# A fused two-block transformer kernel: modulation products on TensorE, weight loads one unit later, and an mLSTM loop fetched ahead through the sync queue

## The chip, the core and the metric

The kernel runs on one core of a Trainium2 chip. The metric is the device time of one launch in microseconds (us), and the time given for a kernel is the median of its runs. PE is TensorE, PEld its weight loads, DVE is VectorE, ACT is ScalarE, POOL is GpSimd, and SP is SyncE, which here does nothing but issue transfers.

## What is computed

The sequence has 512 tokens of width 1024. The first block is a hybrid mixer (a gated delta rule and an mLSTM, each run in both directions over chunks of 64 tokens) with a mixture of experts behind it; the second, run twice, is an attention layer with a feed-forward part. Each block is steered by six modulation vectors, which come from a short vector `c` and a wide matrix:

```
c_act = jax.nn.silu(c.astype(jnp.float32))
...
mod = c_act @ ada_w[l].astype(jnp.float32) + ada_b[l].astype(jnp.float32)
sh1, sc1, gt1, sh2, sc2, gt2 = [m[:, None, :] for m in jnp.split(mod, N_MOD, axis=-1)]
hn = rmsnorm(h_res, norm_mix_g[l]) * (1.0 + sc1) + sh1
h_res = h_res + gt1 * hybrid_mixer(
...
```

In the mixer one wide projection feeds everything; the two branches are computed from it and merged under a gate:

```
proj = jnp.einsum("bsd,de->bse", h, w_in.astype(jnp.float32))
a_qkv, a_z, a_gates, b_qk, b_v, b_o, b_gates, merge = jnp.split(proj, SPLIT_POINTS, axis=-1)
...
o_a = rmsnorm(o_a, gdn_norm_g) * jax.nn.silu(a_z.reshape(bsz, s, N_HEADS_A, HEAD_DIM_A))
...
h_b = head_layernorm(h_b, mlstm_norm_g.astype(jnp.float32).reshape(N_HEADS_B, HEAD_DIM_B))
h_b = (h_b * jax.nn.sigmoid(b_o.reshape(bsz, s, N_HEADS_B, HEAD_DIM_B))).reshape(bsz, s, WIDTH_B)
gate_a, gate_b = jnp.split(jax.nn.sigmoid(merge), 2, axis=-1)
y = (gate_a * jnp.einsum("bse,ed->bsd", o_a, w_branch_a.astype(jnp.float32))
     + gate_b * jnp.einsum("bse,ed->bsd", h_b, w_branch_b.astype(jnp.float32)))
```

## The kernel before

**Products.** Activations lie with features on the partitions and 512 tokens along the free axis. Every weight and every activation of a large product is split into a high and a low part, and a product is three matmuls: high by high, high by low, low by high. A weight tile of 1 MB arrives by a transfer of SP into one of four buffers named `raw`; `_split` takes a unit of 1024 columns out of it, ACT copies it to `whi`, and POOL subtracts to get `wlo` (`lo_pool` says whether POOL, 1, or DVE, 0, does that; it is `(1,)` in the mixer). `unit` hands out the next unit, `_ahead` splits up to two units ahead of it, and `_loads` issues loads while fewer than four tiles are held. The matmuls of such units write PSUM tiles named `pd` (128x512) or `tm` (128x256).

**Main and fill.** The mixer's order is that of the program. `drive` runs a main generator, which earns credit, and spends the credit on steps of a fill generator. The main one is first the gated delta rule, twice (directions: half the heads each time): preparation (`pl`, `ptr`, `pG`), a triangular elimination that is a long row of small DVE operations (`stmp<-L,Tm` and `Tm<-Tm,stmp`, the sweep), a block solve (`pQ`, `pY`, `pw`, `pu`), and a scan over chunks in which PE and DVE take turns (`pS`, `pv`). Then it is the mLSTM loop. The fill is the rest of the wide projection: its results go to DRAM by way of tiles `stg` (`z_d`, `qk_d`, `v_d`, `o_d`, and the merge gates `mg_d`) and are fetched again later. Into the fill `weave` puts a step of the modulation work whenever 4.2 units of fill have gone by.

**Modulation.** `ada` (three groups of eight units here: two of the first block, one of the second) takes a `raw` tile of 1024 by 256 and multiplies row block k by column k of `c`. ACT scales four of the eight blocks in place, DVE multiplies and adds the other four into `adacc`, POOL adds ACT's four together and onto `adacc`, and PE sums over the partitions with a vector of ones (`pa`). At the very start of the kernel `ada_first` already does the same product for one group on PE alone (`pada`, column blocks of 32). The buffer `raw` is free for the next load when POOL is done.

**mLSTM loop.** `mlstm` has 16 steps: four pairs of heads, four blocks of 128 keys. A step multiplies queries and keys (`pqk`), DVE multiplies the result by decay weights (`rowt`), and PE multiplies that with the values (`pm`). The weights of a step are a row fetched from DRAM (`mdram`) and spread over the partitions, masked by POOL (`affine_select`) and put through Exp by ACT. After four steps a pair of heads is normalised, gated with the output gate `og` in `mlstm_out`, transposed (`pht`) and split. The fetches of `rowt` are issued by the scalar queue (ACT's), three steps ahead; `og` is fetched when `mlstm_out` begins. Ahead of them on the scalar queue stands the fetch of `oa`, the result of the first branch, which was stored to DRAM just before. Behind the fill, `branch_in` splits `oa` and `branch_a` multiplies it by `wa`, gate by gate (`mg`); both are steps of the fill too.

Of the kernel before, what the change touches and what calls it, by code (L numbers as in the profile page):

```python
# [175 lines left out]
class Build:  # L176
# [151 lines left out]
    def unit(self, key, sel):  # L328

        i = len(self.order)  # L330
        self.order.append((key, sel))
        if self.order_in is None:
            self.raws = getattr(self, "raws", {})
            if key not in self.raws:
                self.raws = {key: self._load(key)}
            self.ready = getattr(self, "ready", {})
            return (i,) + self._split(i)
        assert self.order_in[i] == (key, sel), (i, self.order_in[i], key, sel)
        self._ahead(i)
        return (i,) + self.ready.pop(i)  # L340
# [116 lines left out]
    def ada(self, w, c, bias, out, groups, eng=None):  # L457
# [3 lines left out]
        for g in groups:  # L461
# [915 lines left out]

    def mlstm(self, mp, qk, v_d, o_d, oh, ol):

# [3 lines left out]
        steps = [(f, a) for f in range(4) for a in range(4)]  # L1383
        rowt = {}

        def fetch(i):
            if i < len(steps):
                f, a = steps[i]
                t = rowt[i] = mp.tile([P, 2, 640], F32, tag="rowt", bufs=5, name="rowt")
                self.dma("scalar", t, self.mdram[2 * f:2 * f + 2, a, :].partition_broadcast(P))  # L1390

        def weights(i):
            if i < len(steps):
                f, a = steps[i]
                t, n = rowt[i], T - P * a
                for d in range(2):
                    dg = t[:, :, T:] if d else t[:, :, 0:P]
                    sg = -1 if d else 1
                    nc.gpsimd.affine_select(dg, dg, pattern=[[0, 2], [sg, P]], compare_op=OP.is_ge, fill=NEG, base=0, channel_multiplier=-sg)
                for hh in range(2):  # L1400
                    for d, r in ((0, t[:, hh, 0:n]), (1, t[:, hh, n:])):
                        self.act(r, r, AF.Exp, bias=self.rcol[:, d, a, 2 * f + hh:2 * f + hh + 1])

        va = mp.tile([P, 4, 8, 65], F32, name="va")
        for i in range(4):
            if i < 3:
                fetch(i)
            self.dma("sync", va[:, i], v_d[:, i])
        self.mlg = self.big_row(mp, "ml_g")
        for i in range(2):  # L1410
            weights(i)
        out = None
        for i in range(len(steps) + 1):
            if i < len(steps):
# [5 lines left out]
                for hh in range(2):  # L1420
                    for d in range(2):
                        _, n, t0 = self.span(d, a)
                        r = rowt[i][:, hh, 0:n] if d == 0 else rowt[i][:, hh, 640 - n:]
                        self.stt(r, pss[hh][:, t0:t0 + n], 0.125, r, OP.mult, OP.mult)
            fetch(i + 3)
            weights(i + 2)
            yield 0.6
            if i > 0:
                f, a = steps[i - 1]
                r = rowt.pop(i - 1)  # L1430
                if a == 0:
                    po = [[self.pc("pm") if hh == 0 else self.pd("pm") for _ in range(2)] for hh in range(2)]
# [7 lines left out]
                if a == 3:  # L1440
# [16 lines left out]
                    self.drain(out)  # L1457
                    out = self.mlstm_out(mp, f, hs, o_d, oh, ol)
            for _ in range(3):
# [4 lines left out]

    def mlstm_out(self, mp, f, hs, o_d, oh, ol):

        nc = self.nc
        sh = [P, 4, 2, 64]
        og = mp.tile([P, 4, P], F32, tag="og", bufs=1, name="og")
        self.dma("sync", og, o_d[:, :, P * f:P * f + P])  # L1470
        sm, ss = [mp.tile([P, 4, 2], F32, tag=f"ls{i}", bufs=2, name="ls") for i in range(2)]
# [45 lines left out]

    def branch_in(self, oa, hi, lo):

        for k in range(4):  # L1520
            self.split(oa[:, k], hi[:, k], lo[:, k])
        yield 0.0
# [1046 lines left out]
    def mixer(self, mod0, mod1, px):  # L2569
# [3 lines left out]
        md = lambda i: mod0[:, 8 * i:8 * i + 8]  # L2573
        ada0 = lambda gs: self.ada("ada0", c1, self.vc("ada_b0"), mod0, gs, nc.gpsimd)
        with tc.tile_pool(name="x0", bufs=1, reuse_waits="tile") as x0:
# [45 lines left out]
        self.marks = set()  # L2621
        ada = self.chain(ada0((1, 2)), self.ada("ada1", c2, self.vc("ada_b1"), mod1, (0,), nc.gpsimd))
        with tc.tile_pool(name="mb", bufs=1, reuse_waits="tile") as mb:
            with tc.tile_pool(name="ms", bufs=1, reuse_waits="tile") as ms:
# [4 lines left out]
                with tc.tile_pool(name="mq", bufs=1, reuse_waits="tile") as mq:  # L2629
# [36 lines left out]
            def place():  # L2666
                ya.extend(self.h_tile(m % 2, 4 + m // 2, F32) for m in range(KD))
                yield 0.0

            with tc.tile_pool(name="mp", bufs=1, reuse_waits="tile") as mp:  # L2670
                oa = mp.tile([P, 4, T], F32, name="oa")
                self.dma("scalar", oa, oa_d)
                fill = self.chain(fill, self.branch_in(oa, hi, lo), place(), self.branch_a("wa", (hi[:, 0:4], lo[:, 0:4]), ya, mg_d, mp, 2))
                fill = self.drive(self.mlstm(mp, qk, v_d, o_d, oh, ol), fill)
                self.drain(fill)
        with tc.tile_pool(name="mr", bufs=1, reuse_waits="tile") as mr:
            with ph:
# [127 lines left out]
```

## Time and profile before

| | |
|---|---|
| median of 3 runs | 2731.18 us (2724.32 to 2737.99) |
| profiled execution | 2728.39 us, its span 2726.6 us |
| PE busy | 2490.4 us, 91% of the span |
| DVE, ACT, POOL busy | 1524.1, 929.5, 957.9 us |
| mixer with the mLSTM loop | from about 60 to 745 us of the span |

The page divides the span in 40 slices; the mixer is slices 2 to 11, where PE is mostly 7 or 8 tenths busy and its granted clock below 1 in most slices, while nearly all slices after the 16th show 9 and 9. Times of a stretch are counted from the start of the span. A wait in brackets is the idle time of an engine just before an instruction, with what ended it. Two records of PE stand for one float32 matmul (`pada`, `pa`, `pm`, `pqk`), one for a matmul of split parts (`pd`, `tm`).

### The profile page before, as it was taken

The numbers are of one execution on the slowest core, as the hardware profiler recorded it, in microseconds if no ns is written. First come the engines' busy times: TensorE is split into PE (matmuls) and PEld (weight loads), VectorE is DVE, ScalarE is ACT, GpSimd is POOL, SyncE is SP. The second block draws the span as 40 slices with busy tenths as digits, with TensorE's granted clock in tenths as the row PEclk, the third lists the DMA queues.
The fourth block names the chain that finished last, engine by engine and source line by source line (L and its number), as shares of the span: only waits on it lengthen the run. The fifth ranks groups of instructions, "written<-read, shape, count | busy, mean of one in ns | idle before, by whom it ended". The sixth has DMA issues, their size and how long they took to land.

```text
span 2726.6 us, 35040 instructions
## 1 busy us (share of the span) xinstructions
PE 2490.4 (91%) x13618; PEld 1843.4 (68%) x13618; DVE 1524.1 (56%) x2483; ACT 929.5 (34%) x1534; POOL 957.9 (35%) x652
## 2 busy tenths in 40 slices
PE   7888888787969999889999999999999999999999
PEld 4676776566634444557777877878757777888887
DVE  4896595354446645564455488884454345452523
ACT  3434233444222211333444432323332344442432
POOL 1454454332320000443553333444332343344443
PEclk8989898788979999999999999999999999999999
DMA  9356465534389974432446146552331225232321
GB/s 264 93 187 180 150 183 179 203 108 136 102 325 357 391 301 146 135 124 93 146 148 201 63 154 201 170 192 89 102 93 47 85 82 189 78 108 80 106 93 62
DMA packets 332299, 419.07 MB, mean 154 GB/s; under 512 B 33608, under 2 KB 275760, under 8 KB 323680
## 3 DMA queue, kind: packets, MB, share of 16 engines
q1 hardware_dynamic: 312848, 377.12, 41.8%
q10 hardware_dynamic: 14624, 25.28, 2.7%
q0 software_dynamic: 4656, 14.35, 1.6%
q8 instruction: 113, 1.85, 0.3%
q14 instruction: 58, 0.48, 0.1%
HBM read 387.66 MB, written 33.23 MB: 154 GB/s over the span
## 4 chain that ended last, share of the span: by engine, by line
PE 45%; DVE 6%; issue 3%; POOL 2%; ACT 2%; DMA 1%; ACTq 0%; POOLq 0%; DVEq 0%
PE pd L199 36%; PE psc L199 2%; DVE adacc L214 2%; PE tm L199 2%; POOL wlo L205 2%; PE ptot L199 1%; DMA raw<-in_w_up 1%; DVE cv L214 1%; PE po L199 1%; DVE h L214 1%; PE prr L199 1%; PE pc L199 1%; PE pz L199 1%; PE pso L199 1%; PE pst L199 1%
## 5 line engine op out<-in xcount | busy, mean ns | idle before, releaser
L205 POOL TENSOR_TENSOR wlo<-raw,whi 128x1024 fp32r<-128x1024 f32 (+3 forms) x317 | 720.6, 2279 | 1219.3 <-ACT whi L196 1069.6
L199 PE MATMUL pd<-h,whi 128*128 128x512 f32 (+1 forms) x3440 | 1098.6, 401 | 32.9 <-DVE stg L214 6.3
L199 PEld LDWEIGHTS pd<-h,whi 128*128 128x128 f32 x3440 | 646.4, 193 | 191.0 <-issue 27.1
L199 PE MATMUL pd<-h,wlo 128*128 128x512 f32 (+1 forms) x1720 | 675.9, 393 | 21.9 <-POOL wlo L205 21.9
L196 ACT ACTIVATE whi<-raw 128x1024 fp32r<-128x1024 f32 (+3 forms) x319 | 313.9, 993 | 260.4 <-PE pd L199 117.2
L199 PEld LDWEIGHTS pd<-h,wlo 128*128 128x128 f32 x1720 | 331.4, 193 | 94.4 <-POOL wlo L205 26.2
L199 PE MATMUL pd<-fyh,whi 128*128 128x512 f32 (+1 forms) x546 | 204.7, 375 | 9.3 <-ACT whi L196 5.3
L214 DVE SCALAR_TENSOR_TENSOR cv<-pd,vec,cv 128x511 f32<-128x511 f32 (+1 forms) x176 | 131.8, 749 | 143.8 <-ACT cv L196 138.3
L199 PE MATMUL pd<-fyh,wlo 128*128 128x512 f32 (+1 forms) x546 | 201.8, 370 | 5.5 <-POOL wlo L205 5.5
L214 DVE SCALAR_TENSOR_TENSOR adacc<-raw,cs,adacc 128x256 f32<-128x256 f32 x288 | 201.5, 700 | 9.4
L199 PE MATMUL pd<-fyl,whi 128*128 128x512 f32 (+1 forms) x546 | 200.8, 368 | 0.2 <-DVE fyl L205 0.2
L214 DVE SCALAR_TENSOR_TENSOR xTl<-pd,mod,xTl 128x512 f32<-128x512 f32 (+1 forms) x73 | 49.4, 683 | 188.5 <-PE pd L199 188.5
L199 PE MATMUL pgB<-gu,xt 128*64 128x512 f32 (+1 forms) x304 | 143.1, 608 | 0.3 <-PEq L1981 0.3
L199 PE MATMUL pgA<-gu,xt 128*64 128x512 f32 (+1 forms) x304 | 143.2, 608 | 0.0
L199 PE MATMUL tm<-whi,h 128*128 128x256 f32 x640 | 130.7, 297 | 8.3 <-ACT whi L196 7.9
L199 PEld LDWEIGHTS pd<-fyh,whi 128*128 128x128 f32 x546 | 104.6, 192 | 40.1 <-ACT whi L196 10.4
L199 PEld LDWEIGHTS pd<-fyh,wlo 128*128 128x128 f32 x546 | 104.4, 191 | 24.3 <-POOL wlo L205 7.5
L199 PEld LDWEIGHTS pd<-fyl,whi 128*128 128x128 f32 x546 | 104.7, 192 | 16.8 <-DVE fyl L205 0.7
L199 PEld LDWEIGHTS tm<-whi,h 128*128 128x128 f32 x640 | 107.2, 200 | 9.6 <-ACT whi L196 8.2
L199 PE MATMUL tm<-wlo,h 128*128 128x256 f32 x320 | 93.9, 293 | 7.7 <-POOL wlo L205 7.6
L196 ACT ACTIVATE cv<-pd,vec 128x512 f32<-128x512 f32 x88 | 68.2, 775 | 94.5 <-PE pd L199 93.9
L214 DVE SCALAR_TENSOR_TENSOR xT<-pb,mod,xT 128x512 f32<-128x512 f32 x128 | 87.0, 742 | 2.1 <-PE pb L199 1.9
(564 smaller groups left out, 3366.9 us busy)
## 6 DMA issues: line engine op xcount, KB each, us to landing
raw<-in_ada SPq DMA_DIRECT2D x64, 1024.0 KB, 5.4
raw<-in_w_in SPq DMA_DIRECT2D x54, 1024.0 KB, 6.7
raw<-in_w_up SPq DMA_DIRECT2D x44, 1024.0 KB, 4.9
gu<-in_wg SPq DMA_DIRECT2D x30, 1024.0 KB, 8.7
gu<-in_wu SPq DMA_DIRECT2D x30, 1024.0 KB, 7.0
dn<-in_wd SPq DMA_DIRECT2D x59, 512.0 KB, 9.7
raw<-in_w_dn SPq DMA_DIRECT2D x16, 1024.0 KB, 5.1
raw<-in_wo SPq DMA_DIRECT2D x12, 1024.0 KB
```

Source lines behind the costliest of these rows:

```text
L196: return self.nc.scalar.activation(out, in_, func, **kw)
L199: return self.nc.tensor.matmul(out, lhsT, rhs, start=start, stop=stop)
L205: return (eng or self.nc.vector).tensor_tensor(out, a, b, op=op)
L214: return (eng or self.nc.vector).scalar_tensor_tensor(out, a, s, b, op0=op0, op1=op1)
```

## The change

First, `ada_mm` takes the place of `ada` for the three groups in the mixer: PE multiplies the `raw` tile by the broadcast column of `c`, eight products in four column blocks of 32, ACT copies the sum out, and PE folds the four blocks (`pa`). The bias is added once for each group. A step of it counts 1.2 in the credit, and comes after 6.0 units of fill instead of two steps after 4.2 each. The `ada` of the later layers is as it was.

Second, `_loads` is called only at the start of `unit`, no longer after each split and after each `done`, in the whole kernel.

Third, in the mLSTM loop the rows are fetched by SP, four steps ahead; the first step's row is fetched, masked and put through Exp before the loop, in a buffer of its own; `og` is fetched a step before it is used, in two buffers; `oa` comes in four quarters in two buffers, by SP, and is split only when the rest of the fill has run; and `wlo` is made by DVE until the fill has ended.

```
@@ _ahead, _loads, done
             self.nsplit += 1
-            self._loads()
...
                 del self.raws[key]
-                self._loads()
@@ new
+    def ada_mm(self, w, c, bias, out, groups):
+        for g in groups:
+            pcol = self.ps.tile([P, T], F32, tag="a", bufs=self.ps_a, name="pa")
+            pend = None
+            for j in range(9):
+                if j < 8:
+                    u = self.unit((w, 0, KD, 2048 * g + 256 * j, 256), ("raw",))
+                    ps = self.pc("pada")
+                    for k in range(KD):
+                        q = 32 * (k % 4)
+                        self.mm(ps[q:q + 32, 0:256], c[:, k:k + 1].to_broadcast([P, 32]), u[1][:, k, :], k < 4, k >= 4)
+                    self.done(u)
+                if pend is not None:
+                    for i in range(2):
+                        self.mm(pcol[:, 2 * j - 2 + i:2 * j - 1 + i], pend[:, i * P:(i + 1) * P], self.wmean)
+                if j < 8:
+                    pend = self.gp.tile([P, 256], F32, tag="adacc", bufs=2, name="adacc")
+                    self.act(pend, ps[:, 0:256], AF.Copy)
+                    yield 1.2
+            s = slice(16 * g, 16 * g + 16)
+            self.stt(out[:, s], pcol[:, 0:16], float(D), bias[:, s], OP.mult, OP.add)
@@ mlstm
+    def mlstm_fetch(self, t, f, a):
+        self.dma("sync", t, self.mdram[2 * f:2 * f + 2, a, :].partition_broadcast(P))
...
-                self.dma("scalar", t, self.mdram[2 * f:2 * f + 2, a, :].partition_broadcast(P))
...
-            fetch(i + 3)
+            fetch(i + 4)
             weights(i + 2)
...
+                if a == 2:
+                    og[f] = mp.tile([P, 4, P], F32, tag="og", bufs=2, name="og")
+                    self.dma("sync", og[f], o_d[:, :, P * f:P * f + P])
@@ branch_in
+        for k in range(2):
+            fetch(k)
+        yield from fill
         for k in range(4):
-            self.split(oa[:, k], hi[:, k], lo[:, k])
+            self.split(ts[k], hi[:, k], lo[:, k])
+            fetch(k + 2)
@@ mixer
-        ada = self.chain(ada0((1, 2)), self.ada("ada1", c2, self.vc("ada_b1"), mod1, (0,), nc.gpsimd))
+        ada = self.chain(self.ada_mm("ada0", c1, self.vc("ada_b0"), mod0, (1, 2)), self.ada_mm("ada1", c2, self.vc("ada_b1"), mod1, (0,)))
...
-                    self.spill_tm("w_in", 3616, 2, o_d), self.spill_fm("w_in", 4160, 16, mg_d), self.mark("end")), ada, 4.2)
+                    self.spill_tm("w_in", 3616, 2, o_d), self.spill_fm("w_in", 4160, 16, mg_d), self.mark("end")), ada, 6.0)
...
+                        g1["first"] = mb.tile([P, 2, 640], F32, tag="rowt0", name="rowt")
+                        self.mlstm_fetch(g1["first"], 0, 0)
+                        yield 0.0
+                        yield 0.0
+                        self.mlstm_weights(g1["first"], 0, 0)
...
-                oa = mp.tile([P, 4, T], F32, name="oa")
-                self.dma("scalar", oa, oa_d)
...
+                lo_pool, self.lo_pool = self.lo_pool, (0,)
```

The order of the instructions shows what moves. On POOL, in the first sweep (the rows from the first elimination to the scan; `Tm` and `S` are tiles of the gated delta rule), the additions of the modulation stood between the low parts of the fill's weights:

```order
 L205 TENSOR_TENSOR wlo<-raw,whi 128x1024 x3
-L205 TENSOR_TENSOR raw<-raw 128x512
-L205 TENSOR_TENSOR adacc<-adacc,raw 128x256 x2
-L205 TENSOR_TENSOR wlo<-raw,whi 128x1024
-L205 TENSOR_TENSOR raw<-raw 128x512
-L205 TENSOR_TENSOR adacc<-adacc,raw 128x256 x2
-L205 TENSOR_TENSOR wlo<-raw,whi 128x1024 x2
-L1156 MEMSET S 128x256
+L1060 MEMSET Tm 128x1024
+L1061 MEMSET Tm 128x32
+L205 TENSOR_TENSOR wlo<-raw,whi 128x1024 x9
+L1178 MEMSET S 128x256
```

Now nothing but low parts stands between the clearing of `Tm` and that of `S`.

On ACT, where the gated delta rule ends and the mLSTM loop begins, the fetches of `oa` and of the first rows stood behind the stores of `oa_d`:

```order
 L217 DMA oa_d<-stg 128x512
-L217 DMA oa<-oa_d 128x2048
-L217 DMA rowt<-mdram 128x2x640 x3
-L196 ACTIVATE rowt<-rowt,rcol 128x512
-L196 ACTIVATE rowt<-rowt,rcol 128x128
```

On SP, at the same place, the rows now go out between the fetches of the values `va`, and the first one has gone out earlier still:

```order
+L217 DMA mg_d<-stg 128x512 x2
+L217 DMA raw<-in_w_in 128x8x256
+L217 DMA va<-v_d 128x520
+L217 DMA rowt<-mdram 128x2x640
+L217 DMA va<-v_d 128x520
+L217 DMA rowt<-mdram 128x2x640
+L217 DMA va<-v_d 128x520
+L217 DMA rowt<-mdram 128x2x640
+L217 DMA va<-v_d 128x520
 L217 DMA row_ml_g<-in_rows 128x512
```

The rows no longer stand behind the fetch of `oa` on any queue.

On SP, at the end of the loop, loads for the merge (`wo`, gates `mg`) gave way to stores of merge gates that are still to be computed and to the second half of `oat`, as `oa` is now called:

```order
-L217 DMA mg<-mg_d 128x512 x2
-L217 DMA raw<-in_wo 128x8x256
+L217 DMA raw<-in_wa 128x4x256
+L217 DMA mg_d<-stg 128x512 x2
+L217 DMA raw<-in_wa 128x4x256
+L217 DMA mg_d<-stg 128x512
+L217 DMA raw<-in_wb 128x4x256
+L217 DMA mg_d<-stg 128x512 x2
+L217 DMA oat<-oa_d 128x512 x2
+L217 DMA mg<-mg_d 128x512 x2
```

So part of the fill has moved behind the loop. Counted in PE's order, 132 `pd` matmuls of the fill that stood ahead of the loop now stand behind it (342 of them between the loop's last transposes and the next sums, 210 before), the loop itself holds as many as it did, and 192 `pada` matmuls (24 units of eight) stand ahead of the loop, where the fill left room. The four reloads of ACT's tables that the loop's last quarter caused (Tanh for the gates, Exp for the rows) are gone from ACT's order.

## Rows read from the trace of the kernel before

**Rows 1.** The page: the span.

```profile
span 2726.6 us, 35040 instructions
```

**Rows 2.** Stretches: length, each engine's busy us (count), PEclk, DMA share, GB/s.

```profile
109.00:253.00 144.00, 114.01 (x1188) 94.32 (x1188) 118.30 (x179) 57.28 (x95) 66.56 (x43) 0.91 0.57 174
253.00:346.00 93.00, 76.85 (x960) 68.80 (x960) 57.65 (x100) 35.09 (x58) 45.72 (x37) 0.93 0.49 153
346.00:490.00 144.00, 122.17 (x1424) 98.10 (x1424) 97.73 (x167) 44.81 (x74) 66.14 (x43) 0.92 0.61 182
490.00:520.00 30.00, 15.16 (x75) 11.91 (x76) 8.37 (x20) 13.98 (x30) 8.31 (x14) 0.66 0.70 249
520.00:632.00 112.00, 92.08 (x446) 68.47 (x446) 55.45 (x137) 54.76 (x112) 37.09 (x42) 0.82 0.35 110
```

**Rows 3.** Stretches, tile adacc alone: length, PE, PEld, DVE, POOL, then as above.

```profile
109.00:253.00 144.00, 4.21 (x32) 4.50 (x32) 24.16 (x36) 14.52 (x16) 0.91 0.57 174
253.00:346.00 93.00, 2.62 (x20) 2.71 (x20) 11.46 (x20) 10.40 (x12) 0.93 0.49 153
346.00:490.00 144.00, 4.42 (x32) 4.41 (x32) 18.43 (x32) 12.16 (x16) 0.92 0.61 182
```

**Rows 4.** Groups from 109 to 490 us: busy, mean ns, idle before.

```profile
L214 DVE SCALAR_TENSOR_TENSOR adacc<-raw,cs,adacc 128x256 f32<-128x256 f32 x66 | 45.9, 696 | 2.4
L205 POOL TENSOR_TENSOR adacc<-adacc,raw 128x256 f32<-128x256 f32 x44 | 37.1, 843 | 54.3 <-DVE adacc L214 51.7
L205 POOL TENSOR_TENSOR raw<-raw 128x512 f32<-128x512 f32 x22 | 32.1, 1461 | 2.1 <-ACT raw L196 2.1
```

**Rows 5.** Timeline around 190 us of DVE, POOL and PE: start, length.

```profile
190.47 0.42 DVE L205 TENSOR_TENSOR Tm<-Tm,stmp 128x247 f32<-128x247 f32 x1
195.62 2.40 DVE L205 TENSOR_TENSOR stmp<-L,Tm 128x220 f32<-128x220 f32 x1
...
193.77 1.56 POOL L205 TENSOR_TENSOR adacc<-adacc,raw 128x256 f32<-128x256 f32 x2 [11.26 <-DVE adacc L214]
195.29 4.96 POOL L205 TENSOR_TENSOR wlo<-raw,whi 128x1024 fp32r<-128x1024 f32 x2
...
197.84 0.79 PE L199 MATMUL pd<-h,wlo 128*128 128x512 f32 x1 [9.17 <-POOL wlo L205]
```

**Rows 6.** Timeline of PE in the first 60 us: products of the first group.

```profile
32.59 1.94 PE L199 MATMUL pada<-wa,crep 128*32 128x256 f32 x16 [4.63 <-DMA wa<-in_ada]
47.76 1.07 PE L199 MATMUL pada<-wa,crep 128*32 128x256 f32 x16
```

**Rows 7.** The chain that ended last: start, length, count.

```profile
1439.36 32.71 PE pd L199 x143
```

**Rows 8.** What SP's queue waited for from 60 to 640 us.

```profile
SPq L217 <- POOL adacc L205: 88.7, 17, 16.4
SPq L217 <- DVE adacc L214: 71.2, 10, 13.1
```

**Rows 9.** ACT's queue at the start of the loop.

```profile
491.05 0.33 ACTq L217 DMA_DIRECT2D oa<-oa_d  x1
492.48 1.51 ACTq L217 DMA_DIRECT2D rowt<-mdram  x3
```

**Rows 10.** What PE waited for from 490 to 632 us.

```profile
PE pm L199 <- DVE rowt L214: 13.3, 1, 13.3
PE pqk L199 <- DVE rowt L214: 9.3, 3, 3.7
PE pht L202 <- DVE hs L205: 6.2, 1, 6.2
```

**Rows 11.** Transfers by the page: KB each, us to landing.

```profile
raw<-in_ada SPq DMA_DIRECT2D x64, 1024.0 KB, 5.4
...
mg<-mg_d SPq DMA_DIRECT2D x16, 256.0 KB, 4.5
```

**Rows 12.** Low parts made by DVE in the first 70 us.

```profile
L205 DVE TENSOR_TENSOR wlo<-raw,whi x2: 1478/2012/2546, 32.2 to 62.8; 128x1024 fp32r<-128x1024 f32 x2
```

More of the change, by code (lines that the diff above doesn't have):

```diff
@@ L1376, in span, with mlstm_weights, mlstm @@
         return self.OFF[d][a], (T - P * a if d == 0 else P * (a + 1)), (P * a if d == 0 else 0)
-    def mlstm(self, mp, qk, v_d, o_d, oh, ol):
+    def mlstm_fetch(self, t, f, a):
+        self.dma("sync", t, self.mdram[2 * f:2 * f + 2, a, :].partition_broadcast(P))
+    def mlstm_weights(self, t, f, a):
+        n = T - P * a
+        for d in range(2):
+            dg = t[:, :, T:] if d else t[:, :, 0:P]
+            sg = -1 if d else 1
+            self.nc.gpsimd.affine_select(dg, dg, pattern=[[0, 2], [sg, P]], compare_op=OP.is_ge, fill=NEG, base=0, channel_multiplier=-sg)
+        for hh in range(2):
+            for d, r in ((0, t[:, hh, 0:n]), (1, t[:, hh, n:])):
+                self.act(r, r, AF.Exp, bias=self.rcol[:, d, a, 2 * f + hh:2 * f + hh + 1])
+    def mlstm(self, mp, mb, first, qk, v_d, o_d, oh, ol):
         nc = self.nc
         steps = [(f, a) for f in range(4) for a in range(4)]
-        rowt = {}
+        rowt = {0: first}
         def fetch(i):
             if i < len(steps):
-                f, a = steps[i]
-                t = rowt[i] = mp.tile([P, 2, 640], F32, tag="rowt", bufs=5, name="rowt")
-                self.dma("scalar", t, self.mdram[2 * f:2 * f + 2, a, :].partition_broadcast(P))
+                rowt[i] = mp.tile([P, 2, 640], F32, tag="rowt", bufs=5, name="rowt") if i % 6 else \
+                    mb.tile([P, 2, 640], F32, tag="rowt0", name="rowt")
+                self.mlstm_fetch(rowt[i], *steps[i])
         def weights(i):
             if i < len(steps):
[L1394 to L1402, printed above, removed]
+                self.mlstm_weights(rowt[i], *steps[i])
         va = mp.tile([P, 4, 8, 65], F32, name="va")
         for i in range(4):
-            if i < 3:
+            if i:
                 fetch(i)
@@ L1409, in mlstm @@
         self.mlg = self.big_row(mp, "ml_g")
-        for i in range(2):
-            weights(i)
-        out = None
+        weights(1)
+        out, og = None, {}
         for i in range(len(steps) + 1):
@@ L1457, in mlstm @@
                     self.drain(out)
[L1458 removed]
+                    out = self.mlstm_out(mp, f, hs, og.pop(f), oh, ol)
             for _ in range(3):
@@ L1463, in mlstm, with mlstm_out @@
         yield from out
-    def mlstm_out(self, mp, f, hs, o_d, oh, ol):
+    def mlstm_out(self, mp, f, hs, og, oh, ol):
         nc = self.nc
         sh = [P, 4, 2, 64]
-        og = mp.tile([P, 4, P], F32, tag="og", bufs=1, name="og")
-        self.dma("sync", og, o_d[:, :, P * f:P * f + P])
         sm, ss = [mp.tile([P, 4, 2], F32, tag=f"ls{i}", bufs=2, name="ls") for i in range(2)]
@@ L1516, in gate_loads, with branch_in, fetch @@
         return get
-    def branch_in(self, oa, hi, lo):
+    def branch_in(self, src, hi, lo, fill):
+        ts = []
+        def fetch(k):
+            if k < 4:
+                ts.append(self.gp.tile([P, T], F32, tag="mt", bufs=2, name="oat"))
+                self.dma("sync", ts[k], src[:, k])
+        for k in range(2):
+            fetch(k)
+        yield from fill
         for k in range(4):
-            self.split(oa[:, k], hi[:, k], lo[:, k])
+            self.split(ts[k], hi[:, k], lo[:, k])
+            fetch(k + 2)
         yield 0.0
@@ L2670, in mixer @@
             with tc.tile_pool(name="mp", bufs=1, reuse_waits="tile") as mp:
-                oa = mp.tile([P, 4, T], F32, name="oa")
-                self.dma("scalar", oa, oa_d)
-                fill = self.chain(fill, self.branch_in(oa, hi, lo), place(), self.branch_a("wa", (hi[:, 0:4], lo[:, 0:4]), ya, mg_d, mp, 2))
-                fill = self.drive(self.mlstm(mp, qk, v_d, o_d, oh, ol), fill)
+                lo_pool, self.lo_pool = self.lo_pool, (0,)
+                fill = self.chain(self.branch_in(oa_d, hi, lo, fill), place(), self.branch_a("wa", (hi[:, 0:4], lo[:, 0:4]), ya, mg_d, mp, 2))
+                fill = self.drive(self.mlstm(mp, mb, g1["first"], qk, v_d, o_d, oh, ol), fill)
                 self.drain(fill)
+                self.lo_pool = lo_pool
         with tc.tile_pool(name="mr", bufs=1, reuse_waits="tile") as mr:
```

1 line of the change is left out of this document (removed).

## The prediction

> **What bounds the kernel now.** I began with the page. The span is 2726.6 us [rows 1], and its slices show two kernels: behind the mixer PE is at nine tenths and its clock mostly at full, while in the mixer it is at seven or eight with the clock below. The change's work lies in the mixer alone, so the second view was the engines' busy time by stretches of it [rows 2]. From 109 to 253 us (preparation, the first sweep and the solve) DVE is busy 118.3 of 144 us and PE 114.0; from 253 to 346 (scan, results, next preparation) PE 76.9 of 93; from 346 to 490 (the second half of the heads) PE 122.2 and DVE 97.7 of 144. So neither engine is full, and both wait for each other. Then the loop: 30 us of start with a clock of 0.66 and PE busy 15.2, and 112 us at 0.82.
>
> The same stretches for the tile `adacc` show what the modulation takes there: 24.2, 11.5 and 18.4 us of DVE, 54.0 in all [rows 3], and 37.1 + 32.1 us of POOL in its two operations [rows 4]. What that does to PE is best read in one place, the timeline at 190 us [rows 5]. DVE is in the sweep, one small operation after the other; the modulation's turn comes late, POOL sits 11.26 us until DVE has delivered `adacc`, and only then makes the low part for which PE sits 9.17 us. An engine with little to do holds up the fill, since it stands in order behind work that waits for the busiest one.
>
> For the loop I read PE's waits [rows 10] and ACT's queue at its start [rows 9]: 13.3 us for the first weighted row. The rows were not asked for until 492.48, as they stood behind the fetch of `oa`, which waited until 491.05 for a store to land.
>
> **The change part by part.** *Products on PE.* The kernel has the same product at its start, so there is a row: a unit (16 records) takes 1.07 us at full clock and 1.94 at half [rows 6]. 24 units are 25.7 us, at most 46.6. Where the fill makes room for them is known: 132 `pd` matmuls leave the stretches ahead of the loop, at 32.71/143 = 0.229 us each [rows 7], 30.2 us. So PE has about 4.5 us less to do there, not more. Its present work is its busy time by its clock, 114.0 x 0.91 + 76.9 x 0.93 + 122.2 x 0.92 = 288 us [rows 2]; 283 would remain, in what are now 381 us. PE does not forbid a gain of up to 98 us.
>
> *Relief of DVE.* The 54.0 us are an upper bound for what leaving DVE can give. The lower one is nothing, if PE's own order sets the pace everywhere. PE and DVE are about equally busy in the three stretches, so I take half: **-27 us (0 to -54)**. ACT's scaling and POOL's sums go too, ACT gets one copy per unit; neither is a bound there (57.3 and 66.6 of 144 us).
>
> *The wait at 197.84.* Its whole chain, `adacc` on DVE, `adacc` on POOL, then the low part, is removed work. I take it in full: **-9 us (0 to -9)**. What is late next is the sweep itself, which I leave where it is. Shorter waits of this kind I leave to the half above.
>
> *Loads issued later.* SP stood 88.7 + 71.2 us behind the modulation [rows 8], because a load was issued where the buffer was not yet free, and all transfers queued behind it waited too, the stores of the fill and the fetches of the solve among them. After the change the load stands behind those. In the layers the order of loads is the same but for a few that slip behind a gate's fetch or the eight fetches of the residual; all are asked for two units or more ahead, about 11 us by 48 x 0.229, against 5.4 us to landing [rows 11]. **0 us.** Without that cover one such load would cost up to 5 us.
>
> *First rows of the loop.* The first one is fetched, masked and exponentiated before the loop, so nothing of the 13.3 us is left for step 0. Rows 1 to 3 stand between the values on SP, ahead of `oa`. I leave 3 us for step 1, whose mask and exponentials still come after its landing. **-10, and -2 for the clock of 0.66: -12 us (-5 to -18).**
>
> *In the loop.* PE waits 9.3 us for rows and 6.2 at the last transposes [rows 10]. The gate `og` is asked for a step earlier, four table loads leave ACT's path at the end, and three units of the modulation leave ACT and DVE. The normalisation chain on DVE stays, so I take 9 of the 15.5. The clock at 0.82, against 0.92 in the stretches ahead, is worth 11 us over 112; I take 5. **-14 us (0 to -22).** Against this stand the low parts on DVE: five or six in the loop at 1.5 to 2.5 us [rows 12], on an engine busy 55 of 112 us. They are hidden unless a row's multiplication queues behind one that waits for its high part; then six by 1.5, **0 us (to +9)**.
>
> *Behind the loop.* The 132 matmuls come back here, where nothing runs beside them: +30.2 us. Then `oa` is split, and its third and fourth quarter are asked for only when the first are done. A transfer of that size takes 4.5 us to landing [rows 11], under which PE has 24 matmuls of the first two quarters at most, and in the first gate only six, 1.4 us. Before, the loop's last steps covered the split. I add 5: **+35 us (+28 to +42).**
>
> Sum: -27 - 9 - 12 - 14 + 35 = **-27 us**, from the profiled 2728.4 to **2701 us**. The median of the runs, 2731.2, is 3 us above the profiled run; I don't add that. All ends together give 2728 - 54 - 9 - 18 - 22 + 28 = 2653 and 2728 - 5 + 42 + 9 = 2774.
>
> The Trainium skill, page "DMA: Bandwidth & Descriptors", section "Issuing engines are not separate DMA queues", says that transfers issued by different engines run on the same 16 DMA engines, and that spreading them saves only the sequencer's time to issue. By that, moving the rows to another queue would give about nothing, and the sum would be -15 us, 2713. The trace neither confirms nor denies the rule; what rows 9 show is lateness of the issue, behind a transfer that itself waited, and this the move takes away.
>
> **The rivals.** *POOL holds DVE, and the gain is larger.* The operation at 195.62 takes 2.40 us, where the one of nearly its size at 190.47 took 0.42, and it lies beside a low part on POOL [rows 5]; and `adacc` itself has a mean of 696 ns on DVE. If any POOL operation holds DVE so, the 69.2 us of the modulation [rows 4] give back DVE time: by their share of `adacc` [rows 3] 27 us fall into the first stretch, where DVE is busy 0.82 of the time, and 23 into the third, at 0.68. If half of DVE's operations are of the kind that is held, that is 11 + 8 = 19 us: 2682. The Trainium skill, page "SBUF — State Buffer", section "Who interferes with whom", has such a rule: a DVE instruction with two inputs in SBUF and a GpSimd one that reads SBUF share a port as an exclusive lock, and the second to come waits. The trace agrees at 195.62. Against a large effect: the low parts stay on POOL ahead of the loop, and they are its longest operations.
>
> *PE is the pace already, no change.* PE's order is fixed, and its waits in the scans are for DVE's answers, not for free time on it. Then the relief gives 10 instead of 36, the loop 4, the start 12, and the fill moved behind costs its 35: +9, 2737. For it speaks PE's share of 0.79 to 0.85 [rows 2] with small matmuls in it; against it the 9.17 us.
>
> *PE waits for modulation weights, slower.* Until now PE saw only finished sums. Now it reads the `raw` tile in its own order, and what stands behind it is the main chain. The load is issued a unit later, behind stores and fetches that wait. At the start PE did wait 4.63 us for such a tile [rows 6]. If 12 of the 24 wait so, that is 56 us: 2757. From 1.1 us a unit in the mean (27/24) the gain is gone, and from 1.7 it is slower than can be measured. Against it: the buffer is free as soon as PE has read it, and the 160 us of rows 8 vanish.
>
> *The rows are late on SP too.* If the stores ahead of them wait for their tiles, the first wait stays: 2711.
>
> **How the numbers follow.** The forecast as summed has 0.52, with a range of its own from 2685 to 2717; the larger gain 0.15; no change 0.17; slower 0.09; rows still late 0.07. The range of 2660 to 2736 takes in all but the slower case and the far end of the larger gain. About 0.5% (14 us) is what a measurement of this kernel can tell from no change. Faster by more holds the forecast, the larger gain and most of the last case, 0.72; within it lies most of "no change", 0.17; slower has 0.11.
>
> **What would show it.** In the changed kernel's profile: `pada` units of 1.1 us without a wait for `raw` between 109 and 490; no `adacc` on DVE and POOL there, and no wait of PE near 9 us in the first sweep; the loop's start, now near 490 us, at 450 to 460, with no 13 us wait; a loop of about 100 us; and from its last transposes to the merge 30 to 40 us more than now. I would be wrong if PE waits for `raw` add up to over 27 us, if the loop starts less than 15 us earlier, or if the time behind the loop grows by more than 42.

## The result, and the profile after

The changed kernel takes 2714.03 us in the median of 10 runs (2705.52 to 2719.40), the kernel before 2728.31 (10 runs, 2718.44 to 2737.99): a ratio of 0.9942, 95% interval 0.9927 to 0.9956. It is faster by some 14 to 16 us, about half of the 27 forecast. The profiled execution took 2710.12 us, its span 2708.4.

The stretches of the changed kernel that answer to [rows 2], cut at four landmarks of the program: the first `pqk` (the loop begins), the first `pm` (its first weighted row is there), the last `pht` (the loop's last transposes), the first `pst` (the merge is done). Columns as in [rows 2].

```profile
109.00:459.00 350.00, 296.10 (x3806) 237.57 (x3806) 207.56 (x355) 105.73 (x158) 100.09 (x54) 0.92 0.62 185
459.00:464.00 5.00, 5.00 (x22) 2.78 (x20) 1.68 (x4) 0.60 (x1) 0.31 (x1) 1.00 0.71 203
464.00:586.00 122.00, 97.11 (x508) 71.81 (x507) 60.55 (x143) 51.88 (x114) 28.46 (x42) 0.85 0.39 126
586.00:685.00 99.00, 87.53 (x346) 67.68 (x345) 43.76 (x49) 33.78 (x48) 14.11 (x6) 0.92 0.47 155
```

The kernel before, cut at the same landmarks:

```profile
109.00:484.00 375.00, 307.35 (x3548) 258.00 (x3548) 273.68 (x445) 136.20 (x225) 176.72 (x121) 0.91 0.56 170
484.00:503.00 19.00, 5.70 (x27) 3.25 (x25) 0.95 (x3) 2.70 (x6) 3.11 (x7) 0.71 0.98 352
503.00:631.00 128.00, 106.22 (x516) 79.43 (x517) 62.65 (x154) 66.74 (x137) 43.17 (x52) 0.81 0.36 117
631.00:698.00 67.00, 57.14 (x215) 44.60 (x214) 29.33 (x34) 20.59 (x32) 21.23 (x9) 0.86 0.48 158
```

Ahead of the loop 25 us are gained, at the first row 14, in the loop 6, and 32 are given back behind it: 13 us at the first `pst`. DVE has 66 us less to do ahead of the loop (273.68 to 207.56), yet PE still sits 350 - 296.10 = 54 us, against 68 before. From the first `pr` of the layers, at 1145.0, to the end are 1563.4 us, where the kernel before has 1569.9 from 1156.7: another 6.5 us, where nothing was forecast.

The products of the modulation are near the size that was forecast: the 23 of the 24 units in this stretch take 26.95 us of PE (25.7 was for all 24), and PE never waits for their tile: no `raw` stands among its waits up to the loop. Stretch of the tile `pada` alone (PE, PEld, DVE, ACT), then the longest of PE's waits (in total, times, longest):

```profile
109.00:459.00 350.00, 26.95 (x368) 10.04 (x368) 0.00 (x0) 8.95 (x24) 0.92 0.62 185
```

```profile
PE pY L199 <- DVE Qs L1116: 11.7, 1, 11.7
PE pa L199 <- ACT adacc L196: 9.2, 2, 7.2
PE pG L199 <- DVE M L205: 8.5, 1, 8.5
PE pl L199 <- ACT sq L196: 8.1, 2, 4.1
```

The wait of 9.17 us for a low part [rows 5] is gone. Three of the four shown are new: for `Qs`, for the copied sum `adacc` and for `M`. The last comes back below; ahead of the other two neither DVE nor ACT has much work. The timelines of ACT, SP, PE and DVE of the changed kernel show what they wait for (start, length; idle time and what ended it in brackets):

```profile
184.93 1.06 ACT L196 ACTIVATE whi<-raw 128x1024 fp32r<-128x1024 f32 x1 [15.36 <-DMA raw<-in_w_in]
185.89 0.64 ACT L196 ACTIVATE adacc<-pada 128x256 f32<-128x256 f32 x2
...
212.19 1.06 ACT L196 ACTIVATE whi<-raw 128x1024 fp32r<-128x1024 f32 x1 [17.05 <-DMA raw<-in_w_in]
213.15 0.37 ACT L196 ACTIVATE adacc<-pada 128x256 f32<-128x256 f32 x1
213.41 0.68 ACT L196 ACTIVATE stg<-pd,vec 128x512 f32<-128x512 f32 x1
```

```profile
177.56 0.37 SPq L217 DMA_DIRECT2D z_d<-stg  x1
178.02 0.42 SPq L217 DMA_DIRECT2D raw<-in_w_in  x1
...
195.36 3.96 SPq L217 DMA_DIRECT2D Xc<-xd  x4
199.37 5.75 SPq L217 DMA_DIRECT2D Y<-yd  x8
205.21 0.43 SPq L217 DMA_DIRECT2D z_d<-stg  x1
205.74 1.30 SPq L217 DMA_DIRECT2D raw<-in_w_in  x1
```

```profile
186.31 1.01 PE L199 MATMUL pa<-wmean,adacc 128*128 128x1 f32 x4 [7.21 <-ACT adacc L196]
```

```profile
214.13 3.10 DVE L214 SCALAR_TENSOR_TENSOR stg<-pd,vec,stg 128x510 f32<-128x510 f32 x4 [17.28 <-ACT stg L196]
217.15 0.68 DVE L1116 COPY Qs<-pQ 128x512 f32<-128x512 f32 x1
```

Read from the last back: PE waits for `Qs`, which stands on DVE behind four operations on `stg`; these wait for ACT's part of `stg`, which stands behind a high part; that waits for its tile, and the tile was asked for at 205.74 only, behind twelve fetches of the solve and a store, and ACT can go on at 212.19. At 177.56 it is the same with a store ahead and the copy of the modulation's sum behind.

From this came two theories for the missing half. **Theory 1:** the late loads stand behind stores and fetches on SP, ACT waits for tiles, and the relief is partly given back. **Theory 2:** the late loads cost nothing or help, and what is missing is the pace of PE and of DVE's chain.

### The profile page after: what moved, and what is told of

Read it like the earlier page. It is cut to its first block, busy times and chain, and to the rows that moved or that the text cites. A ratio compares the mean times of both kernels' runs of the same rounds, so it can differ in the third digit from the quotient of the medians.

```text
span 2708.4 us, 35539 instructions
## 1 busy us (share of the span) xinstructions
PE 2496.3 (92%) x14002; PEld 1840.5 (68%) x14002; DVE 1468.5 (54%) x2400; ACT 895.8 (33%) x1458; POOL 858.5 (32%) x567
## 4 chain that ended last, share of the span: by engine, by line
PE 46%; DVE 6%; issue 3%; ACT 2%; POOL 1%; DMA 1%; ACTq 0%; POOLq 0%; DVEq 0%
PE pd L199 36%; PE psc L199 2%; DVE adacc L214 2%; PE tm L199 2%; POOL wlo L205 1%; PE ptot L199 1%; PE pc L199 1%; PE po L199 1%; DVE h L214 1%; PE pz L199 1%; DMA raw<-in_w_up 1%; DVE cv L214 1%; PE pso L199 1%; PE pst L199 1%; ACT whi L196 1%
## 5 line engine op out<-in xcount | busy, mean ns | idle before, releaser
L205 POOL TENSOR_TENSOR wlo<-raw,whi 128x1024 fp32r<-128x1024 f32 (+3 forms) x304 | 691.3, 2280 | 1349.7 <-ACT whi L196 1324.5
L214 DVE SCALAR_TENSOR_TENSOR adacc<-raw,cs,adacc 128x256 f32<-128x256 f32 x216 | 156.0, 722 | 6.9
```

Of the source, the lines that this page charges most:

```text
L205: return (eng or self.nc.vector).tensor_tensor(out, a, b, op=op)
L214: return (eng or self.nc.vector).scalar_tensor_tensor(out, a, s, b, op0=op0, op1=op1)
```

## The experiments

Medians of 4 to 12 runs, each beside the kernel before on the same chip; the lengths of the stretches are those of one trace each. They can be read to some 7 us only: up to the loop the kernels `e1_early`, `e2_early_mixer` and `e7_soon_to_loop` run the same program, in 337, 345 and 351 us with granted clocks of 0.94, 0.93 and 0.89. PE's idle time there is steadier, 40 to 45 us.

| kernel | median us, ratio (95%) | up to loop | PE idle, clock there | to first `pm` | loop | behind | first `pr` to end |
|---|---|---|---|---|---|---|---|
| before | 2728.3 | 375 | 68, 0.91 | 19 | 128 | 67 | 1570 |
| changed | 2714.0, 0.9942 (0.9927 to 0.9956) | 350 | 54, 0.92 | 5 | 122 | 99 | 1563 |
| e2_early_mixer | 2703.5, 0.9912 (0.9892 to 0.9932) | 345 | 45, 0.93 | 5 | 123 | 104 | 1566 |
| e5_products_only | 2725.7, 0.9993 (0.9974 to 1.0011) | 343 | 43, 0.92 | 18 | 125 | 106 | 1565 |
| e4_loop_only | 2718.0, 0.9963 (0.9944 to 0.9981) | 381 | 67, 0.89 | 8 | 134 | 62 | 1568 |
| e3_late_only | 2710.1, 0.9945 (0.9927 to 0.9963) | 376 | 70, 0.90 | 20 | 123 | 58 | 1559 |
| e7_soon_to_loop | 2700.8, 0.9900 (0.9879 to 0.9920) | 351 | 43, 0.89 | 5 | 120 | 95 | 1560 |
| e1_early | 2713.3, 0.9945 (0.9924 to 0.9966) | 337 | 40, 0.94 | 6 | 120 | 103 | 1565 |
| e6_lo_pool | 2715.5, 0.9961 (0.9946 to 0.9977) | 355 | 53, 0.90 | 5 | 118 | 92 | 1566 |
| e9_fill_back | 2685.1, 0.9852 (0.9830 to 0.9874) | 353 | 32, 0.96 | 5 | 129 | 57 | 1560 |
| e11_credit_only | 2691.3, 0.9868 (0.9849 to 0.9886) | 357 | 35, 0.96 | 5 | 135 | 58 | 1564 |
| e12_products_credit | 2698.0, 0.9886 (0.9868 to 0.9904) | 352 | 31, 0.96 | 17 | 121 | 67 | 1570 |
| e10_more_fill | 2702.3, 0.9902 (0.9886 to 0.9918) | 380 | 32, 0.96 | 25 | 130 | 41 | 1564 |

### Loads early again in the mixer: e2_early_mixer

```
         self.nsplit += 1
+        if self.seg == 'mixer':
+            self._loads()
...
             del self.raws[key]
+            if self.seg == 'mixer':
+                self._loads()
```

> The changed kernel, but in the mixer loads are again issued as soon as a unit is split or done (in the layers they stay late). Theory 1 (the late loads stand behind the stores of the fill on SP, so ACT's copies to the high part wait 15.4 and 17.1 us for their tiles, with the copy of the modulation's sum and the evacuations queued behind them): both waits fall below 5 us, PE's waits before the loop of 11.7 us (for Qs) and 7.2 us (for the copied sum) go, the loop starts 10 to 19 us earlier than at 459, and the time falls from 2714 to 2695 to 2704. Theory 2 (late loads cost nothing or help, since SP no longer stands before a buffer that is not free; the missing gain is PE's own pace and DVE's chain): loop start between 455 and 470, time 2711 to 2722.

2703.5 us: theory 1 by the time. The two waits of PE for `Qs` and for the copied sum are gone from the list, and ACT's waits for weight tiles fall by half. First the changed kernel (109 to 459 us), then this one (109 to 454):

```profile
ACT whi L196 <- DMA raw<-in_w_in: 71.5, 8, 18.3
```

```profile
ACT whi L196 <- DMA raw<-in_w_in: 33.6, 6, 18.3
```

PE's idle time falls by 9 us. But theory 1 had put both waits of ACT below 5 us, and one of 18.3 is left at the same place (until 205.85 us, for a tile asked for at 197.84, now ahead of the fetches); only PE no longer stands behind it. The loop starts only 5 us earlier in this trace instead of 10 to 19, and 104 us lie behind it instead of 99. Its profiled execution was also the longest of its runs (2713.5), so that what it shows against the changed kernel is read from the idle time and from the waits, not from the span.

### One part alone: e5_products_only, e4_loop_only, e3_late_only

Each is the kernel before with one of the three parts of the change, as its diff stands above.

> The kernel before with the first part alone: products of the modulation on PE, a step after 6.0 units of fill; loads early, loop as before. Theory 1: without late loads the relief comes out in full size, first pqk at 445 to 455 instead of 484, behind the loop 30 us come back, time 2728 - 36 + 30 = 2722 (2716 to 2726). Theory 2: the relief is no larger than in the changed kernel (25 us, first pqk at 459 or later), time 2728 - 25 + 30 = 2733 (2729 to 2738).

2725.7, at the far end of theory 1's range. The relief is there in full size, 32 us (375 to 343), and behind the loop come 39 instead of 30. The products on PE alone bring nothing that can be measured (the interval of the ratio holds 1).

> The kernel before with the third part alone: rows, gates and first branch by SP and further ahead, low parts by DVE in the loop; modulation on ACT, DVE and POOL, loads early. Both theories: first rows -12 to -14, in the loop -7 (measured in the changed kernel) to -14 (forecast), the first branch split behind the fill +5; time 2728 - 13 - 7 + 5 = 2713 (2706 to 2718). If the fill that lies in the loop covers less than thought and the split costs over 10, 2718 to 2724.

2718.0, where the first range ends and the second begins, but not for the reason that the second names: behind the loop nothing is lost (62 against 67). The first row comes some 10 us earlier (8 against 19), and the loop itself is no shorter, 134 against 128 in this trace. PE's waits in it, to be held against [rows 10]:

```profile
PE pqk L199 <- DVE rowt L214: 7.6, 3, 3.5
PE pht L202 <- DVE hs L205: 5.5, 1, 5.5
PE pm L199 <- ACT stg L196: 5.1, 1, 5.1
PE pm L199 <- DMA va<-v_d: 3.0, 1, 3.0
```

The 13.3 us are gone; the 9.3 and 6.2 us have become 7.6 and 5.5, with all rows and gates fetched further ahead. Those waits were for DVE's own chain, and the fetches had nothing to do with them.

> The kernel before with the second part alone: loads issued only when the next unit is asked for, in the whole kernel. Theory 1: the stores of the fill delay the loads of the mixer, ACT's high parts wait for tiles 10 us and more in one place or two, time 2728 + 5 to + 15 = 2733 to 2743. Theory 2: SP is no longer held by the modulation's buffers (88.7 + 71.2 us), and the layers gain the 5.4 us seen in the changed kernel: 2715 to 2725.

2710.1: theory 1 is wrong for the kernel before, and theory 2 too small. Up to the loop nothing moves (376 and 375); the loop is 5 us shorter, the stretch behind it 9 and the layers 11. Of the 9, some 5 are idle time of PE (10 to 5 us) and the rest its granted clock (0.86 to 0.93). This part, put at 0 in the prediction, is by the medians the largest of the three when it stands alone. What it does behind the loop shows on SP's queue. First the kernel before, then this one: transfers issued just ahead of the merge, where `in_wo` is the weight of the next product.

```profile
643.11 0.38 SPq L217 DMA_DIRECT2D raw<-in_wo  x1
643.59 1.00 SPq L217 DMA_DIRECT2D mg<-mg_d  x2
653.01 0.38 SPq L217 DMA_DIRECT2D raw<-in_wo  x1
653.48 2.83 SPq L217 DMA_DIRECT2D mg<-mg_d  x3
```

```profile
641.57 0.39 SPq L217 DMA_DIRECT2D raw<-in_wo  x1
642.05 1.83 SPq L217 DMA_DIRECT2D mg<-mg_d  x3
645.19 0.38 SPq L217 DMA_DIRECT2D raw<-in_wo  x1
654.21 0.32 SPq L217 DMA_DIRECT2D mg<-mg_d  x1
```

In the kernel before SP stops from 644.59 to 653.01 in front of a weight load whose buffer a low part on POOL still has to read (8.3 us by its waits), and the gates stand behind a weight that is needed later than they are. PE, in the same kernel behind the loop, waits for a bank that a multiplication by such a gate has yet to read; with late loads that wait is not in the list:

```profile
PE pd L199 <- DVE mg L214: 4.9, 2, 4.2
```

The Trainium skill, page "DMA: Bandwidth & Descriptors", section "Anatomy of one DMA — SWDGE (gpsimd) path", says that any wait for a semaphore is made by the issuing sequencer ahead of the dispatch, and never by the DMA engines. The gap on SP from 644.59 to 653.01 agrees with it: all that stands behind the waiting load in program order waits too, whatever the DMA engines have to do.

### Early up to the loop, late behind it: e7_soon_to_loop, and early everywhere: e1_early

```
     def segment(self, name, ctx):
+        self.soon = name == 'mixer'
...
         self.nsplit += 1
+        if self.soon:
+            self._loads()
...
             del self.raws[key]
+            if self.soon:
+                self._loads()
...
         with tc.tile_pool(name="mp", bufs=1, reuse_waits="tile") as mp:
+            self.soon = False
```

In `e1_early` both lines `self._loads()` stand without a condition.

> The changed kernel with the loads early again ahead of the mLSTM loop only; late from the loop's start on, through the end of the mixer and the layers. Theory 1 (late loads hurt where stores and fetches of the fill stand on SP, and help behind the loop, where a load that waits for its buffer holds the fetch of a merge gate that PE needs): loop start at 454 as with early loads in the whole mixer, from the last transposes to the first pst 98 us instead of 104.6, so 4 to 6 us below the 2703.5 of that kernel: 2697 to 2700. Theory 2 (the 6 us behind the loop are chance of the clock): 2702 to 2706, as that kernel.

> The changed kernel with early loads everywhere, that is the first and third part of the change without the second. If the parts only add up (products 2.5 less, loop 10.2 less than 2728.2): 2715 to 2716. If the late loads in the layers are worth the 5 us that their traces show against the early ones (1563 against 1568 us from the first pr to the end), this kernel is 5 above the one with early loads in the mixer alone: 2708 to 2710. If it comes out at 2703, late loads in the layers are worth nothing.

2700.8 lies between the two cases of its expectation, 2713.3 between the first two of its three. The kernel that is late only behind the loop's start beats both uniform ones, the changed kernel by 13 us and the early one by 12. So late loads cost ahead of the loop about what they bring from there on, and in the change as it stands the two cancel: 2713.3 with early loads, 2714.0 with late ones. Behind the loop 95 us stand against 104, as expected, and against 103 in `e1_early` (whose trace was 9 us faster than its median); the medians of `e7_soon_to_loop` and `e2_early_mixer` alone, which differ in this stretch, lie too close to tell (2700.8 and 2703.5). In the layers the five traces with early loads give 1565 to 1570 us, the eight with late ones 1559 to 1566, means 1567.6 and 1562.9. This difference of 5 us is a mean over single traces; which transfer makes it was not looked into.

### Low parts back on POOL: e6_lo_pool

```
-                lo_pool, self.lo_pool = self.lo_pool, (0,)
+                lo_pool, self.lo_pool = self.lo_pool, (1,)
```

> The changed kernel with the low parts on POOL in the loop too, and to the end of the fill. Forecast (low parts on DVE hidden, 0 us): 2711 to 2717. If their 6 times 1.5 us on DVE stand in the way of the row products: 2705 to 2709, with shorter waits of PE for stg and hs. If low parts on POOL hold DVE by the shared port as at 195.62: 2718 to 2722.

2715.5 against 2714.0, as forecast: where the low parts are made in the loop can't be told from the time. The Trainium skill, page "SBUF — State Buffer", section "Who interferes with whom", would let low parts on POOL hold two-input operations of DVE; no run here shows a cost of that in the time of the loop (118 us with POOL, 122 with DVE).

### The count of a step in the credit: e9_fill_back, e11_credit_only, e12_products_credit

One question was left. The products on PE bring 32 us and cost 39 behind the loop, since each step counts 1.2 in the credit and so 132 matmuls of the fill are put off. Had PE no time for them ahead of the loop?

```
                     self.act(pend, ps[:, 0:256], AF.Copy)
-                    yield 1.2
+                    yield 0.0
```

This edit is made to `e7_soon_to_loop` (as `e9_fill_back`), to the changed kernel (`e11_credit_only`) and to `e5_products_only` (`e12_products_credit`).

> Early loads to the loop, late behind it, and a step of the modulation counts nothing in the credit instead of 1.2, so that the 24 steps (28.8 of credit, 6 matmuls per 1.3, 133 matmuls) push no fill out behind the loop. Theory A (PE ahead of the loop still waits 54 us for others, and more fill goes into these waits): from the last transposes to the first pst 65 to 70 us instead of 98 to 105, loop start later by 15 to 25, net 5 to 15 us below the kernel with early loads to the loop. Theory B (PE's waits sit where no fill is placed; every matmul moved back costs its full time): loop start and later stretch cancel, within 3 us of that kernel.

> The changed kernel with one number altered: a step of the modulation counts 0.0 in the credit, not 1.2; late loads everywhere, as in the change. If the counted step is what cost the change its gain: 132 matmuls come back ahead of the loop for nearly nothing, 2714 - 15.7 = 2698 (2694 to 2703). If the late loads ahead of the loop take that away (more stores and fetches of the fill in front of them): 2703 to 2712.

> The kernel before with the first part alone, a step counting 0.0: products on PE, all fill where it was, loads early, loop as before. If the relief of DVE is worth about 20 us at the same fill: 2725.7 - 16 = 2710 (2705 to 2714), loop start 460 to 465 instead of 484. If the gain needs the third part (rows early) to show: 2718 to 2726.

All three gain more than the likeliest case said: 15.7, 22.7 and 27.7 us from one number. The cleanest pair is the last, the products alone. `e5_products_only`, then `e12_products_credit`, up to the loop and behind it:

```profile
109.00:452.00 343.00, 300.19 (x3808) 240.33 (x3808) 208.69 (x355) 103.79 (x154) 100.11 (x52) 0.92 0.62 184
...
595.00:701.00 106.00, 89.10 (x344) 69.64 (x344) 34.34 (x41) 33.10 (x48) 33.20 (x14) 0.91 0.42 139
```

```profile
109.00:461.00 352.00, 321.09 (x3933) 258.55 (x3933) 212.88 (x358) 109.11 (x160) 112.23 (x57) 0.96 0.63 187
...
599.00:666.00 67.00, 55.97 (x215) 43.25 (x214) 29.30 (x34) 20.58 (x32) 21.26 (x9) 0.90 0.48 158
```

The 132 matmuls stand ahead of the loop again, and the stretch is only 9 us longer. PE's work there, busy time by clock, rises from 300.19 x 0.92 = 276 to 321.09 x 0.96 = 308 us, by 32. Of these, 9 lengthened the stretch and 12 went into idle time (43 to 31); the rest came from a granted clock of 0.96 in place of 0.92: with fewer gaps PE was at its upper level, 2.4 GHz against 1.2, for more of the time. Behind the loop 39 us are saved. The waits of `e9_fill_back` up to the loop show the same:

```profile
PE pl L199 <- ACT sq L196: 4.6, 2, 2.5
PE tm L199 <- POOL wlo L205: 4.1, 2, 3.2
PE pa L199 <- DVE mod L214: 3.8, 1, 3.8
PE pada L199 <- issue: 3.7, 1, 3.7
```

The 8.5 us for `M` are not in the list, nor in those of `e11_credit_only` and `e12_products_credit`, while in all six kernels with the fill put off PE waits 8.1 to 9.9 us there, with late loads and with early ones. In the changed kernel PE sat there because its fill had been put off. The 11.7 us for `Qs` are another matter: early loads alone remove them (`e2_early_mixer`), and with the fill back but late loads 7.5 us of them stay (`e11_credit_only`).

The other two pairs differ. The 132 matmuls lengthen the stretch up to the loop by 2 us (`e7_soon_to_loop` to `e9_fill_back`, 351 to 353) and by 7 (changed to `e11_credit_only`, 350 to 357), and save 38 and 41 us behind the loop; but the loop becomes 9 and 13 us longer, with PE's idle time in it as before (25 to 26 us) and a lower clock, 0.82 for 0.88 and 0.78 for 0.85. `e4_loop_only` has the same long loop (134 us, 0.79), `e12_products_credit` has not (121 us, 0.84): it goes with the third part of the change where the fill is not put off. Why the clock falls there is not shown. Late loads ahead of the loop cost less once the fill is back, 6 us (2691.3 against 2685.1) instead of 13.

### More fill still: e10_more_fill

```
-    def drive(self, main, fill):
+    def drive(self, main, fill, scale=1.0):
...
-            credit += want or 0.0
+            credit += scale * (want or 0.0)
```

It is `e9_fill_back` with a scale of 1.15 in the two stretches of the gated delta rule; the fill then ends before the loop.

> The kernel with the fill put back, and the credit of the two gated-delta-rule stretches times 1.15, by which all fill lies ahead of the loop and the first branch's products come into the loop. If PE's 31 us of idle time ahead of the loop in the kernel with the fill put back can still be filled: loop start later by under 15, 126 matmuls (29 us) fewer behind it, 5 to 15 below its 2685. If PE is now the pace there (busy 319 of 351 us at a clock near 0.96): loop start later by 25 to 29, the same amount saved behind, within 4 us of 2685. If the loop then lacks what covers its waits: 2690 to 2700.

2702.3, 2 us beyond the third case. The loop starts 27 us later and PE's idle time ahead of it stays (32 us), so that there PE is now the pace, as the second case has it; and the loop's start is 20 us longer. Start and loop of this kernel, then PE's longest wait in them:

```profile
489.00:514.00 25.00, 9.66 (x22) 4.43 (x20) 4.97 (x9) 10.50 (x18) 3.83 (x10) 0.52 0.74 257
514.00:644.00 130.00, 97.85 (x479) 72.46 (x478) 61.97 (x147) 68.33 (x124) 22.91 (x32) 0.76 0.32 102
```

```profile
PE pd L199 <- ACT h L196: 15.3, 2, 13.6
```

PE waits 13.6 us at the loop's start for the split of `oa`: its fetches go out only in the loop, from 496.96 us on, and the products that need it come at once, as no fill is left ahead of them. More fill together with an earlier fetch of `oa` was not tried.

So the filling by the old count, that of `e9_fill_back`, is near the best of the three that were tried. At 2685.1 us, a ratio of 0.9852 (0.9830 to 0.9874), it beats both kernels: some 42 us under the kernel before, 29 under the changed one. Its profiled execution was the shortest of its five (2673.9), so its stretches flatter it somewhat.

## Why the prediction was right, and where it was not

**Right in the whole.** Faster, 2714 within the range of 2660 to 2736 and within the forecast's own 2685 to 2717. None of the three conditions for being wrong came about: no waits for `raw`, the loop 25 us earlier, 32 us more behind it. The gain was half of the 27, and its parts were less well met than the sum; that the sum held is in part luck, since the late loads, whose two effects were not foreseen, cancel nearly to nothing. Two of the signs failed: the loop takes 122 us, not about 100, and in place of the wait of 9 us stand others of 7 to 12.

**The relief of DVE and the wait at 197.84: -36 forecast, -25 measured.** The term was right for what it describes. With early loads PE's idle time up to the loop is 40 to 45 us and the stretch 337 to 351, 24 to 38 less than before (`e1_early`, `e2_early_mixer`, `e5_products_only`, `e7_soon_to_loop`); the late loads add about 10 us of idle time. What the step left out is that part of this gain is only fill put off: at the same fill the products start the loop 375 - 352 = 23 us earlier (`e12_products_credit`).

**Loads issued later: 0 forecast, about 0 in the sum, and wrong in its parts.** The step saw that a load would stand behind stores and fetches, and looked for PE's waits for `raw`. The waits came one engine away: ACT copies a tile to its high part in order, and the evacuations stand behind it. Nor did it see the other side, that a load issued early holds up the gates behind it on SP. Ahead of the loop late loads cost, behind it they gain; `e1_early` and the changed kernel differ by 0.7 us, while on the kernel before, where there was no cost ahead, the late loads alone bring 15 to 18 us (`e3_late_only`, 2710.1).

**First rows of the loop: -12 forecast, -14 measured**, some -10 alone. The forecast gave a chance of 0.07 to rows that are late on SP too; that did not come. What was saved is the wait behind `oa` on the issuing queue, not the time of a transfer; whether the fetch of the first row ahead of the loop would have done it on the old queue too was not tried.

**In the loop: -14 forecast, -6 measured, and that part of the change alone gave nothing** (128 to 134 us). The failed step took 9 of 15.5 us of waits as if the fetches had caused them. They were DVE's multiplication and its normalisation, and both stayed in `e4_loop_only`. In the changed kernel PE idles no less in the loop than before (122 - 97.11 = 25 us against 128 - 106.22 = 22); the 6 us come from 9 us less busy time, at a clock of 0.85 in place of 0.81 and without the modulation's last sums. That the low parts cost nothing on DVE held.

**Behind the loop: +35 forecast, +32 measured**, and +39 without the late loads. The count of 132 matmuls was exact. But the prediction took their move as the price of the products. It is the price of the number 1.2, and could be had back for 2 to 9 us ahead of the loop.

**The rivals.** "PE is the pace already" is refuted by `e12_products_credit`: 32 us of work more on PE up to the loop cost 9 us of time. The larger gain by POOL leaving DVE alone did not come, and the traces bound it: without `adacc`, DVE is busy up to the loop for 220, 213 and 217 us where the modulation is on POOL and DVE (kernel before, `e3_late_only`, `e4_loop_only`), and for 213, 215 and 215 at the same fill with the products on PE (`e12_products_credit`, `e9_fill_back`, `e11_credit_only`). The means differ by 2 us, less than the spread; the rival wanted 19.

## What to carry to other kernels

When work moves onto an engine that interleaves a main chain with fill, ask what the schedule takes away in return: here a step's count in the credit pushed out as much fill as the step added, and the gain of moving 66 us off DVE was lost behind the loop until the count was set to zero. Judge that by the idle time in the stretch (68, 43 and 31 us in the kernel before, `e5_products_only` and `e12_products_credit`) and not by its length, since an earlier start may be put-off work. And a transfer in an ordered queue has two costs, its own lateness and that of all behind it: issue early where stores and fetches would come ahead of it, late where it would wait for a buffer in front of something needed sooner.

## What the runs showed of the hardware

Matmuls put into the gaps of a chain raised the granted clock of the whole stretch up to the loop: with the products on PE it was 0.89 to 0.94 in the six kernels with 132 fewer, and 0.96 in all four that kept them there. It went with PE's idle time and not with the matmuls alone: the kernel before has them there too, with 68 us of idle time and a clock of 0.91. In the other direction, at the loop's start, where PE stood for 13.6 us in `e10_more_fill`, the clock was 0.52, and with rows and fill at hand 1.00 (`e9_fill_back`, as in the changed kernel). I had counted fill at its matmuls' time alone, 30 us; in gaps ahead of the loop it cost 2 to 9 us.
